# Weaving the steps of seven-product pairs, and making the FFN's token sums one stage earlier

## The chip, the cores and the metric

The kernel runs on one core of a Trainium2 chip. A core has a matmul engine (TensorE, PE in the profile, with its weight loads as PEld), a vector engine (VectorE, DVE), an activation engine (ScalarE, ACT), a general engine (GpSimd, POOL) and an engine that here only issues DMAs (SyncE, SP). Each engine works through its own queue of instructions in order, and semaphores make an instruction wait for another engine's. The metric is the time of one execution of the whole kernel on the device, in microseconds (us); lower is better.

## The reference

One encoder block on 256 tokens of width 2048, in fp32: RMSNorm, one wide projection, three attention mixers (A, B, C), a gate for each of them, an output projection, then a SwiGLU feed-forward network (FFN) with 5632 hidden columns. What matters here:

```
h = rms_norm(x, g_mix);  proj = h @ w_in          # queries, keys, values and 3 x 2048 gate columns
merged = sigmoid(gate0) * (oa @ w_br_a) + sigmoid(gate1) * (ob @ w_br_b) + sigmoid(gate2) * (oc @ w_br_c)
x = x + merged @ w_o
hf = rms_norm(x, g_ffn) @ w_ffn_in                # (2048, 2 x 5632)
x = x + (silu(hf[:, :5632]) * hf[:, 5632:]) @ w_ffn_out
```

## The kernel before

**Split products.** Every fp32 matrix is split into a rounded part and a rest, and one product of a 128x128 token tile with a 128x512 weight tile is three matmuls: hi x hi, hi x lo, lo x hi. The weights come from memory as tiles `raw` of 128 rows x (2 x 512) columns, 512 KB each, loaded by SP into a pool of six. ScalarE copies the rounded part (`whi`, L108), VectorE subtracts it from the weights (`wlo`, L109); both have four tiles. The function `halves` does that. So for every weight tile: DMA, ScalarE, VectorE, then TensorE, and a fifth split waits until TensorE is done with the first.

**Pairs.** From the gates on, the work goes by pairs of 512-column blocks (`pair`). The 2048 rows of a weight matrix are eight units of two 128-row tiles. In an ordinary unit each of the two blocks is one step of four products (12 matmuls). In a *seven-product pair* three of the eight units (the table `SEVEN`) are computed with seven products in place of eight, from sums of weights and sums of token tiles. The steps of a pair, with the letters used below (the number is the unit):

- d, D: an ordinary unit's first and second block; 12 matmuls each
- f: a seven-product unit's first step: loads two raw tiles, splits the first; products into the banks X and Y; 6 matmuls
- g: VectorE makes three weight sums (into t3, the second raw tile, t2; L428 to L430) and splits the result; products with token sums into W and Z; 6 matmuls
- h: VectorE makes one more sum in the first raw tile (L444) and half a split; one product into V; 3 matmuls
- p0, p2 and q0, q2: the sums t2 and t3 of all three units are split and multiplied with token sums into X; 6 and 3 matmuls

So a seven-product pair has 61 products, 183 matmuls. After the last f, ScalarE copies bank X to a tile SA; after the last g, bank W to SB; after p2, X again (L379). At the end of a pair VectorE adds banks and copies (L386, L387), while the next pair's steps go on. The token sums that g, p and q need (`stationary_forms`, tiles fh and fl) are six additions (L696), four differences (L699 to L702) and a split, made once for all gate pairs and once for all FFN pairs.

**Order.** A list of steps sets the order in a pair: `ORDER` (`d0 s4 d1 s5 d2 s6 6 d3 7 d7`, where s is f, g, h, and 6 and 7 are p and q) and `ORDER0` for the first gate pair and the first FFN pair. The splits of a step are issued three steps ahead of its matmuls (`AHEAD`). TensorE's and SP's queues keep the program's order; for ScalarE, VectorE and GpSimd the scheduler of the framework orders the queue by an estimated timeline and by priorities. Jobs on the side (evacuations, transposes, sums) advance one step after each step of a pair.

**Stages.** Pairs in order: four gate pairs (seven-product), each followed by an ordinary pair of a branch; two ordinary w_o pairs; the FFN in three blocks: four, four and three seven-product pairs, each block followed by two ordinary pairs of the output. Each 512 columns of the w_o output are added to x, squared and summed, and transposed into a token tile `x1T` of four k-tiles (L760, L111, L112); after the fourth one the token sums of the FFN are started (L764).

Of the kernel before, what the change touches and what calls it, by code (L numbers as in the profile page):

```python
# [57 lines left out]
class InOrder:  # L58

# [16 lines left out]
    def __init__(self, tc):  # L76
        self.tc, self.on = tc, False
        for name in ("tensor", "sync"):
            setattr(self, name, self._Engine(self, getattr(tc.nc, name)))
        for name in ("vector", "scalar", "gpsimd"):  # L80
            setattr(self, name, getattr(tc.nc, name))


@with_exitstack
def encoder_block(ctx: ExitStack, tc: tile.TileContext, a: dict, out: bass.AP):
# [244 lines left out]
    def halves(*srcs):  # L330

        hi = wp.tile([P, PK, NC], F32R, name="whi", bufs=4)
        lo = wp.tile([P, PK, NC], F32R, name="wlo", bufs=4)
        n = 0
        for v in srcs:
            if len(v.shape) == 2:
                split(hi[:, n], lo[:, n], v)
                n += 1
            else:
                split(hi[:, n:n + v.shape[1]], lo[:, n:n + v.shape[1]], v)  # L340
                n += v.shape[1]
        return hi, lo

    def pair(src, lhs, order, done, forms=None, operand=None):
# [33 lines left out]
        def copy(to, b):  # L378
            nc.scalar.activation(tl[to[0]][:, to[1]], ps[b], AF.Copy)  # L379
# [10 lines left out]
        def whole(u, c):  # L390
            def ready():
# [33 lines left out]
        def second(u):  # L425
            def ready():
                b1, b2 = held[u]
                nc.vector.tensor_add(t3[:, SEVEN.index(u)], b2[:, 0], b2[:, 1])  # L428
                nc.vector.tensor_add(b2[:, 0], b2[:, 0], b1[:, 0])
                nc.vector.tensor_add(t2[:, SEVEN.index(u)], b2[:, 0], b2[:, 1])  # L430
                hi, lo = halves(b2)

                def products():
                    mul("W", forms(u, 0), hi[:, 0], lo[:, 0])
# [4 lines left out]
            return ready

        def third(u):
            def ready():
                b1 = held.pop(u)[0]
                nc.vector.tensor_add(b1[:, 1], t2[:, SEVEN.index(u)], b1[:, 1])  # L444
# [24 lines left out]
        steps = []  # L469
        for o in order:  # L470
            u = int(o[1:] or 0)
            steps += {"d": lambda: [whole(u, 0), whole(u, 1)], "s": lambda: [first(u), second(u), third(u)],
                      "6": lambda: [rest("6", v) for v in range(0, seven, 2)],
                      "7": lambda: [rest("7", v) for v in range(0, seven, 2)]}[o[0]]()
# [27 lines left out]
    whole_k = lambda n: ["d%d" % u for u in range(n)]  # L502
# [205 lines left out]
    def merging():  # L708
        forms = stationary_forms(xT, tail)
        for b, (g0, k0, k1) in enumerate(((8, 2, 6), (4, 6, 12))):  # L710
            for j in (0, 2):
# [25 lines left out]
                yield pair(block_pair(a["w_gate"], g0 + j), xT, ORDER if b + j else ORDER0, gates, forms)  # L737
# [7 lines left out]
    def projecting():  # L745
# [4 lines left out]
        for n in (0, 2):  # L750
            def add(c, r, n=n):
# [4 lines left out]
                def later():  # L756
# [18 lines left out]
    def feeding():  # L775
        for c0, c1 in ((0, 4), (4, 8), (8, KF // 4)):
            hT = []
            for n in range(c0, c1):
# [19 lines left out]
                yield pair(lambda u, c, n=n: a["w_ffn"][n][2 * u + c], x1l, ORDER0 if n == 0 else ORDER, hidden,  # L798
# [107 lines left out]
```

## Time and profile before

| | |
|---|---|
| three runs, median (lowest to highest) | 1429.26 us (1427.81 to 1429.84) |
| the profiled execution | 1429.38 us, its span on the core 1427.6 us |
| granted TensorE clock, mean | 0.995 |
| data moved | 277.06 MB at a mean of 194 GB/s |

Stages by the profile's time, from the span's start: the three attention mixers and their projections until 377 us, gate and branch pairs until 607, the two w_o pairs until 698, then the FFN. A row of busy times by stretch gives the stretch, its length, then busy time and count of instructions for PE, PEld, DVE, ACT and POOL, the granted clock (1.00 is full), the DMA share and GB/s. A row of the timeline gives start, duration, engine, line, operation, tiles written and read, shapes, count, and in brackets the idle time before it with what ended it. A row of a group gives how often, the summed busy time, the mean in ns, and the idle time before. A row of waits gives the total, the number and the longest, in us. Buffer numbers are left out of tile names, so t2 and t3 both read t.

### The profile page before, as it was taken

The numbers are of one execution on the slowest core, as the hardware profiler recorded it, in microseconds if no ns is written. First come the engines' busy times: TensorE is split into PE (matmuls) and PEld (weight loads), VectorE is DVE, ScalarE is ACT, GpSimd is POOL, SyncE is SP. The second block draws the span as 40 slices with busy tenths as digits, with TensorE's granted clock in tenths as the row PEclk, the third lists the DMA queues.
The fourth block names the chain that finished last, engine by engine and source line by source line (L and its number), as shares of the span: only waits on it lengthen the run. The fifth ranks groups of instructions, "written<-read, shape, count | busy, mean of one in ns | idle before, by whom it ended". The sixth has DMA issues, their size and how long they took to land.

```text
span 1427.6 us, 17323 instructions
## 1 busy us (share of the span) xinstructions
PE 1397.1 (98%) x6287; PEld 1145.9 (80%) x6287; DVE 1026.0 (72%) x1305; ACT 767.6 (54%) x1026; POOL 76.6 (5%) x146
## 2 busy tenths in 40 slices
PE   8999999999999999999979999999999999999998
PEld 6778878888877888888858888888888888888886
DVE  5767756765578878755779987547988845788854
ACT  6766545654465564545456566335566643456632
POOL 0024532200000000000000000000000000000000
PEclk9999999999999999999999999999999999999999
DMA  8975535455555566755536656655565665565634
GB/s 295 335 243 197 158 123 173 163 163 193 175 192 192 182 219 188 264 179 184 170 119 207 208 188 215 185 190 192 197 199 180 225 189 191 180 201 188 220 128 174
DMA packets 79413, 277.06 MB, mean 194 GB/s; under 512 B 8992, under 2 KB 11552, under 8 KB 79072
## 3 DMA queue, kind: packets, MB, share of 16 engines
q1 hardware_dynamic: 79184, 275.94, 58.9%
q8 instruction: 49, 0.80, 0.2%
q14 instruction: 36, 0.29, 0.1%
q10 hardware_dynamic: 144, 0.02, 0.0%
HBM read 273.05 MB, written 2.88 MB: 193 GB/s over the span
## 4 chain that ended last, share of the span: by engine, by line
PE 83%; DVE 6%; DMA 5%; POOL 2%; issue 2%; ACT 2%; SPq 0%; DVEq 0%; ACTq 0%; POOLq 0%
PE mm L70 17%; PE mmZ L70 14%; PE mmV L70 14%; PE mmY L70 14%; PE mmQ L70 12%; PE mmX L70 6%; DVE wlo L109 3%; DMA raw<-in_w_gate 2%; PE mmW L70 2%; PE tp L70 1%; ACT whi L108 1%; DMA raw<-in_w_mem 1%; PE sc L70 1%; POOL rot L561 1%; DMA rows<-in_mem 1%
## 5 line engine op out<-in xcount | busy, mean ns | idle before, releaser
L109 DVE TENSOR_TENSOR wlo<-raw,whi 128x1024 fp32r<-128x1024 f32 (+1 forms) x541 | 636.9, 1191 | 305.7 <-ACT whi L108 303.5
L108 ACT ACTIVATE whi<-raw 128x1024 fp32r<-128x1024 f32 (+1 forms) x541 | 549.0, 1025 | 552.4 <-PE mmQ L70 159.3
L70 PE MATMUL mm<-whi,xT 128*128 128x512 f32 x768 | 244.8, 395 | 0.0
L70 PEld LDWEIGHTS mm<-whi,xT 128*128 128x128 f32 x768 | 144.6, 190 | 29.7 <-issue 0.8
L70 PE MATMUL mm<-wlo,xT 128*128 128x512 f32 x384 | 151.3, 394 | 0.0
L70 PE MATMUL mmY<-whi,x1T 128*128 128x512 f32 x286 | 112.4, 393 | 0.0
L70 PE MATMUL mmV<-whi,x1T 128*128 128x512 f32 x286 | 111.9, 391 | 0.0
L70 PE MATMUL mmZ<-whi,x1T 128*128 128x512 f32 x220 | 85.8, 390 | 0.0
L70 PE MATMUL mmQ<-whi,x1T 128*128 128x512 f32 x220 | 85.6, 389 | 0.0
L70 PEld LDWEIGHTS mm<-wlo,xT 128*128 128x128 f32 x384 | 72.8, 190 | 15.8 <-issue 0.8
L109 DVE TENSOR_TENSOR wlo<-t,whi 128x1024 fp32r<-128x1024 f32 (+1 forms) x60 | 55.9, 953 | 19.2 <-ACT whi L108 19.0
L70 PE MATMUL mmZ<-whi,hT 128*128 128x512 f32 x176 | 69.6, 396 | 0.0
L70 PE MATMUL mmQ<-whi,hT 128*128 128x512 f32 x176 | 69.1, 392 | 0.0
L70 PE MATMUL mmV<-whi,hT 128*128 128x512 f32 x176 | 69.0, 392 | 0.0
L70 PE MATMUL mmY<-whi,hT 128*128 128x512 f32 x176 | 69.0, 392 | 0.0
L70 PEld LDWEIGHTS mmV<-whi,x1T 128*128 128x128 f32 x286 | 54.0, 189 | 11.5
L70 PEld LDWEIGHTS mmY<-whi,x1T 128*128 128x128 f32 x286 | 53.9, 188 | 10.8
L108 ACT ACTIVATE whi<-t 128x1024 fp32r<-128x1024 f32 (+1 forms) x60 | 50.0, 841 | 13.7 <-PE mmQ L70 13.7
L70 PE MATMUL mmY<-wlo,x1T 128*128 128x512 f32 x143 | 56.0, 391 | 0.0
L70 PE MATMUL mmV<-wlo,x1T 128*128 128x512 f32 x143 | 55.9, 391 | 0.0
L428 DVE TENSOR_TENSOR t<-raw 128x512 f32<-128x512 f32 x45 | 31.1, 691 | 30.8 <-DMA raw<-in_w_ffn 15.4
L70 PEld LDWEIGHTS mmQ<-whi,x1T 128*128 128x128 f32 x220 | 41.3, 188 | 8.6
(252 smaller groups left out, 2548.8 us busy)
## 6 DMA issues: line engine op xcount, KB each, us to landing
raw<-in_w_ffn SPq DMA_DIRECT2D x176, 512.0 KB, 3.9
raw<-in_w_gate SPq DMA_DIRECT2D x96, 512.0 KB, 3.9
raw<-in_w_ffn_out SPq DMA_DIRECT2D x88, 512.0 KB, 3.6
raw<-in_w_qkv SPq DMA_DIRECT2D x64, 512.0 KB, 4.6
raw<-in_w_o SPq DMA_DIRECT2D x32, 512.0 KB, 3.6
raw<-in_w_br SPq DMA_DIRECT2D x24, 512.0 KB, 3.7
raw<-in_w_mem SPq DMA_DIRECT2D x16, 512.0 KB, 6.7
rawT<-in_memT SPq DMA_DIRECT2D x8, 256.0 KB, 5.2
```

Source lines behind the costliest of these rows:

```text
L70: ins = op(*args, **kw)
L108: nc.scalar.activation(hi, src, AF.Copy)
L109: nc.vector.tensor_sub(lo, src, hi.bitcast(F32))
L428: nc.vector.tensor_add(t3[:, SEVEN.index(u)], b2[:, 0], b2[:, 1])
L561: op(ov[:, :, :, c], ov[:, :, :, c], tmp[:, :n])
```

## The change

- `SEVEN` is (1, 2, 3) in place of (4, 5, 6), and the order lists now name single steps, so that f, g, h of a unit can stand apart, with d or D steps of other units between. There are three lists: one for the first gate pair, one for the first FFN pair, one for all others.
- `follow`: splits of weights and sums of weights on VectorE, and splits on ScalarE, each get a dependency on the one issued before on the same engine, so that these keep the program's order. The scheduler places everything else around them.
- The copies of banks X and W are issued with high priority.
- The FFN's token sums are started after the second 512 columns of w_o, since units 1 to 3 need only token tiles 2 to 7.

```diff
-SEVEN = (4, 5, 6)
-ORDER = "d0 s4 d1 s5 d2 s6 6 d3 7 d7".split()
-ORDER0 = "d0 d1 d2 s4 d3 s5 s6 6 7 d7".split()
+SEVEN = (1, 2, 3)
+STEPS = "d0 f1 D0 g1 d4 h1 f2 D4 g2 d5 h2 f3 D5 g3 d6 h3 p0 p2 D6 q0 q2 d7 D7".split()
+STEPS_GATE = "d0 D0 d4 D4 f1 d5 g1 D5 h1 f2 g2 d6 h2 f3 g3 h3 p0 p2 D6 q0 q2 d7 D7".split()
+STEPS_FFN = "d0 D0 f1 d4 g1 D4 h1 f2 d5 g2 D5 h2 f3 d6 g3 h3 p0 p2 D6 q0 q2 d7 D7".split()
...
+    def follow(self, ins):
+
+        if self.on:
+            last = self.before.get(ins.ins.engine)
+            if last is not None:
+                self.tc.add_manual_dep(ins.ins, last, mybir.DependencyInfo(mybir.DependencyClass.NoSync,
+                                                                           mybir.DependencyReason.DATA),
+                                       reason="follow")
+            self.before[ins.ins.engine] = ins.ins.name
...
-            if len(v.shape) == 2:
-                split(hi[:, n], lo[:, n], v)
-                n += 1
-            else:
-                split(hi[:, n:n + v.shape[1]], lo[:, n:n + v.shape[1]], v)
-                n += v.shape[1]
+            v = v.unsqueeze(1) if len(v.shape) == 2 else v
+            o = slice(n, n + v.shape[1])
+            nc.follow(nc.scalar.activation(hi[:, o], v, AF.Copy))
+            nc.follow(nc.vector.tensor_sub(lo[:, o], v, hi[:, o].bitcast(F32)))
+            n += v.shape[1]
...
         def copy(to, b):
-            nc.scalar.activation(tl[to[0]][:, to[1]], ps[b], AF.Copy)
+            with tc.high_priority():
+                nc.scalar.activation(tl[to[0]][:, to[1]], ps[b], AF.Copy)
...
-                    if u + 1 < len(order):
+                    if 2 * u + 2 < KT:
...
-                nc.vector.tensor_add(t3[:, SEVEN.index(u)], b2[:, 0], b2[:, 1])
-                nc.vector.tensor_add(b2[:, 0], b2[:, 0], b1[:, 0])
-                nc.vector.tensor_add(t2[:, SEVEN.index(u)], b2[:, 0], b2[:, 1])
+                nc.follow(nc.vector.tensor_add(t3[:, SEVEN.index(u)], b2[:, 0], b2[:, 1]))
+                nc.follow(nc.vector.tensor_add(b2[:, 0], b2[:, 0], b1[:, 0]))
+                nc.follow(nc.vector.tensor_add(t2[:, SEVEN.index(u)], b2[:, 0], b2[:, 1]))
...
-                yield pair(block_pair(a["w_gate"], g0 + j), xT, ORDER if b + j else ORDER0, gates, forms)
+                yield pair(block_pair(a["w_gate"], g0 + j), xT, STEPS if b + j else STEPS_GATE, gates, forms)
...
-                    if n + c == 3:
+                    if n + c == 1:
                         forms.append(stationary_forms(x1l))
+                    elif n + c == 3:
                         yield 2
...
-                yield pair(lambda u, c, n=n: a["w_ffn"][n][2 * u + c], x1l, ORDER0 if n == 0 else ORDER, hidden,
+                yield pair(lambda u, c, n=n: a["w_ffn"][n][2 * u + c], x1l, STEPS if n else STEPS_FFN, hidden,
```

The places in the queues that matter, before and in the changed kernel. The line numbers move by 10 to 13 (L108 becomes L121 or, in `halves`, L351; L109 becomes L122 or L352).

ScalarE in the first gate pair, before, from the split of h5 to that of q2 (the tiles t_3605 and t_3606 are t2 and t3):

```order
L108 ACTIVATE whi<-raw 128x512
L108 ACTIVATE whi<-raw 128x1024 x2
L379 ACTIVATE SA<-mmX 128x512
L108 ACTIVATE whi<-raw 128x512
L108 ACTIVATE whi<-t_3605 128x1024
L108 ACTIVATE whi<-t_3605 128x512
L379 ACTIVATE SB<-mmW 128x512
L108 ACTIVATE whi<-t_3606 128x1024
L108 ACTIVATE whi<-t_3606 128x512
```

and in the changed kernel, from the split of h2 to that of D6:

```order
L351 ACTIVATE whi<-raw 128x512
L351 ACTIVATE whi<-raw 128x1024
L392 ACTIVATE SA<-mmX 128x512
L351 ACTIVATE whi<-raw 128x1024
L351 ACTIVATE whi<-raw 128x512
L351 ACTIVATE whi<-t_3605 128x1024
L392 ACTIVATE SB<-mmW 128x512
L351 ACTIVATE whi<-t_3605 128x512
L351 ACTIVATE whi<-raw 128x1024
```

The copy of X now stands between the splits of f3 and g3, no longer behind that of g6, and a split of raw (D6) stands between those of t2 and t3.

VectorE where the FFN's token sums end, before, in the first FFN pair (ffull are the six sums, fraw the differences, fl the split's rest):

```order
L699 TENSOR_TENSOR fraw<-ffull 128x384
L109 TENSOR_TENSOR wlo<-raw,whi 128x1024
L428 TENSOR_TENSOR t_6054<-raw 128x512
L701 TENSOR_TENSOR fraw<-fraw,ffull 128x384
L429 TENSOR_TENSOR raw<-raw 128x512
L702 TENSOR_TENSOR fraw<-fraw,ffull 128x384
L430 TENSOR_TENSOR t_6053<-raw 128x512
L109 TENSOR_TENSOR fl<-fraw,fh 128x1536
L109 TENSOR_TENSOR wlo<-raw,whi 128x1024 x2
```

and in the changed kernel, in the second w_o pair:

```order
L706 TENSOR_TENSOR ffull<-x1T 128x256
L709 TENSOR_TENSOR fraw<-ffull 128x384
L352 TENSOR_TENSOR wlo<-raw,whi 128x1024
L711 TENSOR_TENSOR fraw<-fraw,ffull 128x384
L712 TENSOR_TENSOR fraw<-fraw,ffull 128x384
L352 TENSOR_TENSOR wlo<-raw,whi 128x1024
L122 TENSOR_TENSOR fl<-fraw,fh 128x1536
L352 TENSOR_TENSOR wlo<-raw,whi 128x1024 x7
```

The sums now stand among the splits of w_o weights; the split fl is followed by seven splits of weights, of w_o and of the first FFN pair, and only then by the additions of the last w_o blocks to x.

VectorE at the start of the third FFN pair (t_6840 is t3, t_6839 is t2, hT the evacuated transposes of the pair before), before:

```order
L386 TENSOR_TENSOR SB<-mmZ,SB 128x512
L387 TENSOR_TENSOR SB<-mmQ,SB 128x512
L444 TENSOR_TENSOR raw<-t_6839,raw 128x512
L428 TENSOR_TENSOR t_6840<-raw 128x512
L109 TENSOR_TENSOR wlo<-raw,whi 128x1024
L793 TENSOR_TENSOR SA<-SA,SB 128x1024
L429 TENSOR_TENSOR raw<-raw 128x512
L109 TENSOR_TENSOR wlo<-raw,whi 128x512
L109 TENSOR_TENSOR wlo<-raw,whi 128x1024
L430 TENSOR_TENSOR t_6839<-raw 128x512
```

and in the changed kernel:

```order
L399 TENSOR_TENSOR SB<-mmZ,SB 128x512
L400 TENSOR_TENSOR SB<-mmQ,SB 128x512
L442 TENSOR_TENSOR raw<-raw 128x512
L804 TENSOR_TENSOR SA<-SA,SB 128x1024
L443 TENSOR_TENSOR t_6839<-raw 128x512
L352 TENSOR_TENSOR wlo<-raw,whi 128x1024 x2
L457 TENSOR_TENSOR raw<-t_6839,raw 128x512
L122 TENSOR_TENSOR hT<-tp,hT 128x512
L352 TENSOR_TENSOR wlo<-raw,whi 128x512
L352 TENSOR_TENSOR wlo<-raw,whi 128x1024 x2
```

Before, the sums of the next unit (L428, L429) and the sum for h (L444) ran ahead of splits that stand earlier in the program; now each stands between the splits of its neighbouring steps.

More of the change, by code (lines that the diff above doesn't have):

```diff
@@ L76, in __init__ @@
     def __init__(self, tc):
-        self.tc, self.on = tc, False
+        self.tc, self.on, self.before = tc, False, {}
         for name in ("tensor", "sync"):
@@ L335, in halves @@
         for v in srcs:
-            if len(v.shape) == 2:
-                split(hi[:, n], lo[:, n], v)
-                n += 1
-            else:
-                split(hi[:, n:n + v.shape[1]], lo[:, n:n + v.shape[1]], v)
-                n += v.shape[1]
+            v = v.unsqueeze(1) if len(v.shape) == 2 else v
[3 more added lines that the diff above has]
+            n += v.shape[1]
         return hi, lo
     def pair(src, lhs, order, done, forms=None, operand=None):
-        seven = sum(o[0] == "s" for o in order)
+        seven = sum(o[0] == "f" for o in order)
         left = {"X": 3 * seven}
         for o in order:
-            for b in {"s": "YZWV", "d": "YVZQ" * 2}.get(o[0], ""):
+            for b in {"f": "Y", "g": "WZ", "h": "V", "d": "YV" * 2, "D": "ZQ" * 2}.get(o[0], ""):
                 left[b] = left.get(b, 0) + 1
@@ L443, in ready @@
                 b1 = held.pop(u)[0]
-                nc.vector.tensor_add(b1[:, 1], t2[:, SEVEN.index(u)], b1[:, 1])
+                nc.follow(nc.vector.tensor_add(b1[:, 1], t2[:, SEVEN.index(u)], b1[:, 1]))
                 hi, lo = halves(b1[:, 1])
@@ L449, in rest @@
         def rest(o, v):
-            tt, f = {"6": (t2, 1), "7": (t3, 3)}[o]
+            tt, f = (t2, 1) if o == "p" else (t3, 3)
             n = min(2, seven - v)
@@ L459, in products @@
                     if v + n == seven:
-                        if o == "6":
+                        if o == "p":
                             copy(("B", 0), "X")
@@ L467, in rest @@
             return ready
[L469 to L474, printed above, removed]
+        kinds = {"d": lambda u: whole(u, 0), "D": lambda u: whole(u, 1), "f": first, "g": second, "h": third,
+                 "p": lambda v: rest("p", v), "q": lambda v: rest("q", v)}
+        steps = [kinds[o[0]](int(o[1:])) for o in order]
         for i, ready in enumerate(steps):
@@ L500, in run @@
         nc.on = False
-    whole_k = lambda n: ["d%d" % u for u in range(n)]
+    whole_k = lambda n: [d + str(u) for u in range(n) for d in "dD"]
     block_pair = lambda w, n: lambda u, c: w[n + c][u]
```

## The prediction

> **What bounds the kernel now.** I read the page first, then TensorE's own waits, then the busy time of each stretch between two pairs, then the rows around the longest wait.
>
> ```profile
> span 1427.6 us, 17323 instructions
> PE 1397.1 (98%) x6287; PEld 1145.9 (80%) x6287; DVE 1026.0 (72%) x1305; ACT 767.6 (54%) x1026; POOL 76.6 (5%) x146
> ...
> 781.80 2.04 PE mmX L70 x9
> ```
>
> TensorE is the bound, but its 98% counts matmuls that overlap. The last row, from the chain of waits, is the better measure: nine matmuls in 2.04 us, 0.2267 us each when nothing waits. A seven-product pair has 61 products of three matmuls, 183, so its floor is 41.49 us, plus its transposes. Each stretch below is one pair: the four gate pairs, the second w_o pair, FFN pairs 0, 2 and 10.
>
> ```profile
> 377.25:423.12 45.87, 43.10 (x185) 33.89 (x183) 35.36 (x42) 24.53 (x29) 0.00 (x0) 1.00 0.55 174
> 434.00:477.27 43.27, 41.88 (x184) 34.28 (x183) 34.68 (x41) 24.80 (x29) 0.00 (x0) 1.00 0.57 188
> 488.15:530.69 42.54, 41.94 (x184) 34.20 (x183) 34.69 (x41) 24.80 (x29) 0.00 (x0) 1.00 0.59 192
> 547.01:590.48 43.47, 43.47 (x201) 35.85 (x199) 36.97 (x45) 26.74 (x33) 0.00 (x0) 1.00 0.60 193
> 652.57:698.34 45.77, 45.77 (x210) 37.63 (x208) 25.34 (x29) 22.49 (x32) 0.00 (x0) 1.00 0.57 184
> 698.34:753.64 55.30, 46.53 (x201) 36.86 (x199) 45.07 (x75) 29.26 (x40) 0.00 (x0) 0.94 0.42 134
> 796.60:839.28 42.68, 42.68 (x193) 35.06 (x191) 36.88 (x44) 25.20 (x31) 0.00 (x0) 1.00 0.60 192
> 1313.18:1355.63 42.45, 42.45 (x193) 35.13 (x191) 36.08 (x42) 26.12 (x32) 0.00 (x0) 1.00 0.62 207
> ```
>
> The first number is the length, the third busy time that of VectorE (DVE), the fourth that of ScalarE (ACT). FFN pair 10 (eight transposes, 42.45) has no wait that matters; pair 2 has 0.23. So the FFN's ordinary pairs can give almost nothing. What can be won: gate pairs 45.87, 43.27 and 42.54 against 41.49, so 4.4, 1.8 and 1.1; the fourth (16 transposes, 2.0 more) nothing; and FFN pair 0, 55.30 against 41.49 and about 1.8 for 16 transposes: 12.0. The waits say what ends them:
>
> ```profile
> PE mmW L70 <- ACT fh L108: 6.8, 1, 6.8
> PE mmY L70 <- DVE wlo L109: 2.7, 4, 1.4
> PE mmX L70 <- ACT SB L379: 1.9, 2, 0.9
> ```
>
> ```profile
> 717.74 0.39 PE L70 MATMUL mmY<-whi,x1T 128*128 128x512 f32 x1
> 724.92 0.79 PE L70 MATMUL mmW<-whi,fh 128*128 128x512 f32 x1 [6.79 <-ACT fh L108]
> ...
> 728.58 0.63 PE L70 MATMUL mmV<-whi,x1T 128*128 128x512 f32 x1
> 729.01 0.63 PE L70 MATMUL mmV<-wlo,x1T 128*128 128x512 f32 x1
> ...
> 730.30 0.39 PE L70 MATMUL mmY<-whi,x1T 128*128 128x512 f32 x1
> 730.53 0.39 PE L70 MATMUL mmV<-whi,x1T 128*128 128x512 f32 x1
> ```
>
> In FFN pair 0 TensorE stands from 717.74 to 724.92 because the token sums (tile fh) are made late; the next matmuls start 0.43 us apart (728.58 to 729.01) instead of 0.23. The nine matmuls from 724.92 to 729.83 took 4.9 us instead of 2.04. Wait (6.95) and slow spell (2.87) cost 9.8 of the 12.0; the other 2.2 are short waits near the pair's end.
>
> **The change part by part.** No matmul, load or sum is added or removed; TensorE's floor stays. The changed bound on the operand fetch in the first pair means the same eight units, so that stage stays as it is.
>
> *Token sums.* The six additions, four differences and the split move from FFN pair 0 into the second w_o pair.
>
> ```profile
> L109 DVE TENSOR_TENSOR wlo<-raw,whi 128x1024 fp32r<-128x1024 f32 x31 | 37.9, 1223 | 25.5 <-ACT whi L108 25.2
> L696 DVE TENSOR_TENSOR ffull<-x1T 128x256 f32<-128x256 f32 x6 | 2.5, 418 | 0.0
> L701 DVE TENSOR_TENSOR fraw<-fraw,ffull 128x384 f32<-128x384 f32 x1 | 0.6, 554 | 0.0
> L109 DVE TENSOR_TENSOR fl<-fraw,fh 128x1536 fp32r<-128x1536 f32 x1 | 1.8, 1757 | 0.9 <-ACT fh L108 0.9
> L108 ACT ACTIVATE fh<-fraw 128x1536 fp32r<-128x1536 f32 x1 | 1.5, 1482 | 4.1 <-DVE fraw L702 4.1
> ```
>
> That is 2.5 + 4 x 0.55 + 1.76 = 6.5 us of VectorE and 1.5 of ScalarE. The w_o pair has VectorE busy 25.34 of 45.77 us and ScalarE 22.49, so 20 and 23 idle: hidden, 0. Were that cover gone, 6.5. Nothing waits behind them: in the new order the last of them, the split into fh and fl, stands after the eleventh of this pair's sixteen weight splits. Gain: 9.8, all of it if the new first FFN pair has its operands. It reaches token tiles 8 and 9 at its fourth step (d4), before at its seventh:
>
> ```profile
> 703.63 0.48 DVE L112 SCALAR_TENSOR_TENSOR x1T<-tp,gT,x1T 128x256 fp32r<-128x256 f32 x1
> 704.65 0.49 DVE L112 SCALAR_TENSOR_TENSOR x1T<-tp,gT,x1T 128x256 fp32r<-128x256 f32 x1
> ```
>
> These two are ready at 705.1 even in the old queue. The new pair needs them after d0, D0, f1 and three transpose groups: 698.34 + 2.72 + 2.72 + 1.36 + 3 x 0.4 = 706.4. Cover 1.3 us; cost 0.
>
> *Prices for the queues.* Rows of one tail of FFN pair 2, and two of its DVE work:
>
> ```profile
> 822.73 0.39 PE L70 MATMUL mmW<-whi,fl 128*128 128x512 f32 x1
> ...
> 821.18 1.06 ACT L108 ACTIVATE whi<-t 128x1024 fp32r<-128x1024 f32 x1 [0.90 <-PE mmQ L70]
> 822.14 0.58 ACT L379 ACTIVATE SA<-mmX 128x512 f32<-128x512 f32 x1
> 822.62 0.62 ACT L108 ACTIVATE whi<-t 128x512 fp32r<-128x512 f32 x1
> 823.16 0.60 ACT L379 ACTIVATE SB<-mmW 128x512 f32<-128x512 f32 x1
> ...
> 804.94 0.68 DVE L430 TENSOR_TENSOR t<-raw 128x512 f32<-128x512 f32 x1
> 805.54 1.22 DVE L109 TENSOR_TENSOR wlo<-raw,whi 128x1024 fp32r<-128x1024 f32 x1
> 806.68 0.68 DVE L109 TENSOR_TENSOR hT<-tp,hT 128x512 fp32r<-128x512 f32 x1
> ...
> 822.27 1.83 DVE L109 TENSOR_TENSOR wlo<-t,whi 128x1024 fp32r<-128x1024 f32 x2 [1.27 <-ACT whi L108]
> ```
>
> VectorE advances by 0.60 for 512 columns and 1.14 for 1024. ScalarE advances by 0.96 and 0.48, hands over 0.03 after its end (822.24 to 822.27), and copies a bank 0.43 after the start of its last matmul (822.73 to 823.16). I put 0.12 on a VectorE sum that ScalarE waits for, an estimate between that 0.03 and 0.43. On TensorE d and D take 2.72, f, g, p0 and q0 1.36, h, p2 and q2 0.68.
>
> *First gate pair.* The new order has f3, g3, h3, p0 in a row, and ScalarE's row shows the SA copy before g3's split. From f3's start: X's last matmul starts at 0.45, the copy at 0.88, g3's whi at 1.36 to 2.42, its wlo 2.45 to 3.67. TensorE wants g3 at 1.36: wait 2.27 (the wlo is first needed by the second matmul). Then h3 needs an addition (0.60), 0.12, whi 0.62, wlo 0.69: 0.7 late; p0, behind h3 on both engines, 0.8 late. Sum 3.8 against 4.4 now: gain 0.6. So this pair hardly profits, though D6 now stands between p2 and q0 and covers the SB copy (the 1.9 of the third wait row).
>
> *Other gate pairs.* Their waits now sit at D3, d2 and the like, where VectorE was late. In the new order I followed VectorE from the pair's start: eight ops of the merge (4.8) fall before g1, then g1, d4, h1, f2, D4 follow at 1.14 to 2.95 each. It reaches g2 0.13 late and g3, whose two sums, hand-over, whi and wlo take 3.6 against TensorE's 2.72 for D5, 0.45 late; the end 0.07. So 0.65 for pairs two and three (1.8 and 1.1 now: gains 1.1 and 0.4), and 0.5 for the fourth, which has none now: loss 0.5.
>
> *FFN pair 0.* Its tail f3, d6, g3, h3, p0 has d6 between, so g3 is in time; h3 0.5 and p0 0.8 late as above, g2 0.3. 1.6 in place of 2.2: gain 0.6.
>
> *FFN pairs 1 to 10.* VectorE's busy time stays at 36 to 37 of 42.5. What is new is that weight sums and splits keep one sequence, so a sum whose data are there no longer runs ahead. Followed from the pair's start as above, with transposes of the previous pair inside: g2 is 0.3 us early, g3 0.15 late in the eight pairs with transposes, nothing in the two that follow an output pair. 1.2 in all, against about 1.6 now (0.2 to 0.5 in pairs 1, 2, 3, 7 and 9): gain 0.4.
>
> *Loads.* f takes two of the six raw tiles and keeps one until h, now four steps later instead of two. In the new program a load waits for the split five or six steps earlier, before six or seven.
>
> ```profile
> raw<-in_w_ffn SPq DMA_DIRECT2D x176, 512.0 KB, 3.9
> ...
> 443.91 5.76 DMA raw<-in_w_gate
> ```
>
> The tightest is D5, issued when D4's wlo ends; ScalarE asks for it about 7.6 us later. 3.9 at the median, 5.8 the longest piece on the chain: hidden, 0.
>
> Sum: 9.8 + 0.6 + 1.1 + 0.4 - 0.5 + 0.6 + 0.4 = 12.4; I take 12.0, since the small terms rest on waits of tenths. The profiled execution took 1429.38 (the span of 1427.6 and 1.8 around it), so 1417.4. The median of three is 0.12 lower: **1417.3**. Bounds: if every wait of the walk vanished (3.8 + 1.3 + 0.5 + 1.6 + 1.2 = 8.4), 1409; if the token sums alone gained and every other pair lost 0.6, 1425.
>
> **The rivals.** *A, forecast: 1417.3.* Between 1415 and 1420.
>
> *B: the weaving clears the tails too.* For it: VectorE is idle 6 us in each pair. Against: the copy stands before g3 in ScalarE's queue. Half of the 8.4: 1413.
>
> *C: the fixed sequence costs more.* Every sum now waits for the split before it. If VectorE enters each pair 0.6 later than I walked it, the 13 pairs after the first gate pair and FFN pair 0 lose 0.6 each: 7.8, 1425. Against: their VectorE idle time.
>
> *D: the clock.* A gap of 7.18 us was followed by matmuls 0.43 apart. The first gate pair now has one wait of 2.3; if that is enough, it starts a slow spell like the one from 724.92 (nine matmuls with 0.2 us extra each, 1.8): 1419.1. [...]
>
> *E: slower.* Loads come too late. Place: D4, D5, d6 of each pair; price: each us past the 7.6 delays D5's wlo, and with it, in fixed order, all sums behind it. At a landing of 8.1 us, 0.5 in 39 units: 19.5 more than the forecast, 1437. It decides from 7.6; the longest seen is 5.8.
>
> *F: the gain of FFN pair 0 is not there.* The sums are early, but the token tiles of the third w_o block are late by the same 9.8: 1427. Against: the cover of 1.3.
>
> **How the numbers follow.** A 0.55, B 0.12, C 0.17, D 0.06, E 0.05, F 0.05. The range leaves out B's lower half, C's upper half, E and F, together 0.2: 1412 to 1424. For this kernel 0.2% (2.9 us) is about what can be told from no change. Faster (under 1426.4): A, B, D and most of C, 0.88. Same: a quarter of C, and most of F, 0.07. Slower: E, 0.05.
>
> **What would show it.** FFN pair 0 about 45 us long, without the wait on fh and without matmuls 0.43 apart. The second w_o pair still 45.8. The first gate pair about 45.3, with one wait of some 2.3 us before mmW near its end and shorter ones at mmV and mmX. FFN pairs 1 to 10 within 0.3 of 42.5. I am wrong if the first gate pair comes near 42 (B), if ordinary pairs are 43 or more (C), if matmuls wait for DMA (E), or if the fourth step of FFN pair 0 waits for x1T (F).

## The result, and the profile after

The changed kernel takes 1418.5 us (median of four runs, 1417.93 to 1419.69) against 1429.26 (1427.81 to 1429.84, four runs): a ratio of 0.9927, 95% interval 0.991 to 0.9945. It is faster by 10.8 us, close to the forecast of 1417.3. The profiled executions differ by 9.7 us (1429.38 and 1419.69; the spans are 1427.6 and 1417.9).

The head of the page of the changed kernel, then the busy time by stretch, for the same eight stretches as in the prediction: the four gate pairs, the second w_o pair, FFN pairs 0, 2 and 10:

```profile
span 1417.9 us, 17330 instructions
PE 1395.6 (98%) x6287; PEld 1144.8 (81%) x6287; DVE 1033.6 (73%) x1305; ACT 764.9 (54%) x1026; POOL 76.7 (5%) x146
```

```profile
377.32:423.07 45.75, 44.03 (x184) 35.10 (x183) 36.07 (x42) 24.65 (x29) 0.00 (x0) 0.96 0.58 174
433.95:476.16 42.21, 41.90 (x185) 34.27 (x183) 37.02 (x44) 24.43 (x29) 0.00 (x0) 1.00 0.62 199
487.04:529.26 42.22, 41.88 (x184) 34.28 (x183) 37.01 (x44) 24.43 (x29) 0.00 (x0) 1.00 0.62 198
545.58:589.32 43.74, 43.74 (x201) 35.85 (x199) 39.28 (x48) 26.37 (x33) 0.00 (x0) 1.00 0.60 198
651.41:697.18 45.77, 45.77 (x210) 37.64 (x208) 31.45 (x40) 23.87 (x33) 0.00 (x0) 1.00 0.58 184
697.18:742.34 45.16, 44.29 (x200) 35.79 (x199) 39.57 (x64) 29.19 (x41) 0.00 (x0) 1.00 0.53 174
785.22:828.09 42.87, 42.74 (x192) 35.06 (x191) 37.95 (x45) 25.59 (x32) 0.00 (x0) 1.00 0.62 195
1303.06:1345.94 42.88, 42.76 (x192) 35.06 (x191) 37.93 (x45) 25.61 (x32) 0.00 (x0) 1.00 0.60 197
```

By these pairs nearly the whole gain is one row: FFN pair 0 went from 55.30 to 45.16 us. The second w_o pair carries the token sums now (VectorE 31.45 us busy, before 25.34) and still takes 45.77. The first gate pair hardly moved (45.87 to 45.75), and its granted clock is 0.96, where it was 1.00 before. FFN pairs 2 and 10 are longer than before (42.68 and 42.45). Branch and output pairs are the same to 0.05 us.

### The profile page after: what moved, and what is told of

It reads as the page before. It is cut to its first block, busy times and chain, and to the rows that moved or that the text cites. A ratio compares the mean times of both kernels' runs of the same rounds, so it can differ in the third digit from the quotient of the medians.

```text
span 1417.9 us, 17330 instructions
## 1 busy us (share of the span) xinstructions
PE 1395.6 (98%) x6287; PEld 1144.8 (81%) x6287; DVE 1033.6 (73%) x1305; ACT 764.9 (54%) x1026; POOL 76.7 (5%) x146
## 4 chain that ended last, share of the span: by engine, by line
PE 84%; DVE 5%; ACT 3%; issue 3%; DMA 2%; POOL 2%; SPq 0%; ACTq 0%; DVEq 0%; POOLq 0%
PE mm L73 17%; PE mmZ L73 15%; PE mmV L73 14%; PE mmY L73 14%; PE mmQ L73 13%; PE mmX L73 6%; DVE wlo L352 3%; ACT whi L351 2%; PE mmW L73 2%; DMA raw<-in_w_mem 1%; PE tp L73 1%; PE sc L73 1%; POOL rot L571 1%; DVE raw L442 1%; DVE t L441 1%
## 5 line engine op out<-in xcount | busy, mean ns | idle before, releaser
L352 DVE TENSOR_TENSOR wlo<-raw,whi 128x1024 fp32r<-128x1024 f32 (+1 forms) x441 | 509.6, 1168 | 249.1 <-ACT whi L351 245.0
L351 ACT ACTIVATE whi<-raw 128x1024 fp32r<-128x1024 f32 (+1 forms) x441 | 437.4, 1013 | 403.0 <-PE mmV L73 133.7
L122 DVE TENSOR_TENSOR wlo<-raw,whi 128x1024 fp32r<-128x1024 f32 x100 | 128.5, 1295 | 80.8 <-ACT whi L121 80.6
L121 ACT ACTIVATE whi<-raw 128x1024 fp32r<-128x1024 f32 x100 | 105.7, 1070 | 88.1 <-PE mm L73 81.4
L73 PE MATMUL mmV<-whi,x1T 128*128 128x512 f32 x286 | 108.6, 392 | 0.0
L73 PEld LDWEIGHTS mmY<-whi,x1T 128*128 128x128 f32 x286 | 53.7, 188 | 11.3
L352 DVE TENSOR_TENSOR wlo<-t,whi 128x1024 fp32r<-128x1024 f32 (+1 forms) x60 | 54.7, 953 | 3.9 <-ACT whi L351 3.9
L351 ACT ACTIVATE whi<-t 128x1024 fp32r<-128x1024 f32 (+1 forms) x60 | 48.5, 834 | 0.0
```

Source lines behind the costliest of these rows:

```text
L73: ins = op(*args, **kw)
L121: nc.scalar.activation(hi, src, AF.Copy)
L122: nc.vector.tensor_sub(lo, src, hi.bitcast(F32))
L351: nc.follow(nc.scalar.activation(hi[:, o], v, AF.Copy))
L352: nc.follow(nc.vector.tensor_sub(lo[:, o], v, hi[:, o].bitcast(F32)))
```

## The experiments

Each is the changed kernel with one edit, unless it says otherwise. Ratios are against the kernel before, on the same chip, with their 95% interval; the length of a pair is read between the starts of the first matmuls of neighbouring pairs.

**1. The token sums alone, in the kernel before.**

```diff
-SEVEN = (4, 5, 6)
-ORDER = "d0 s4 d1 s5 d2 s6 6 d3 7 d7".split()
+SEVEN = (1, 2, 3)
+ORDER = "d0 s1 d4 s2 d5 s3 6 d6 7 d7".split()
...
-                    if n + c == 3:
+                    if n + c == 1:
                         forms.append(stationary_forms(x1l))
```

The first gate pair gets the list `d0 d4 d5 s1 d6 s2 s3 6 7 d7`, FFN pair 0 the one above.

> The kernel before with one part of the change alone: the seven-product pairs are 1, 2 and 3, and the token sums start in the first w_o pair; no step is woven, no high priority, no following. Theory A (my terms: the gain is the wait of 6.95 us on the token sums and the 2.87 us that the slow matmuls behind it cost): 55.30 us of FFN pair 0 become 42.7 to 45.5, everything else stays within 0.5 us a pair, so the time is about 1419 us (1417 to 1421). Rival (the weaving brings the gain, the early sums only move the wait elsewhere): FFN pair 0 keeps 52 us or more, or the w_o pairs grow by what it loses, and the time is above 1426 us.

1425.18 us (1420.84 to 1430.63), ratio 0.9969 (0.9954 to 0.9983). Neither theory: FFN pair 0 took 50.96 us:

```profile
697.16:748.12 50.96, 45.27 (x201) 37.04 (x200) 38.38 (x62) 29.27 (x40) 0.00 (x0) 0.97 0.46 147
```

The wait on fh is gone, but in its place TensorE stood 2.8 us before f1's first matmul and 2.9 before a transpose, both for splits of token tiles (x1T), which hold the banks that come next. That is the rival F of the prediction, with another cause: the tiles' source was there, their splits stood late in ScalarE's and VectorE's queues. So the early sums by themselves are worth 4.3 us in this pair, not 10.

**2. The weaving, with sums started late.** The start of the sums goes back behind the last w_o half, and FFN pair 0 gets three whole units ahead of its first f.

```diff
-STEPS_FFN = "d0 D0 f1 d4 g1 D4 h1 f2 d5 g2 D5 h2 f3 d6 g3 h3 p0 p2 D6 q0 q2 d7 D7".split()
+STEPS_FFN = "d0 D0 d4 D4 d5 D5 f1 g1 h1 f2 d6 g2 h2 f3 D6 g3 h3 p0 p2 q0 q2 d7 D7".split()
...
-                    if n + c == 1:
+                    if n + c == 3:
                         forms.append(stationary_forms(x1l))
```

> The changed kernel with the token sums started again behind the last w_o half, and in FFN pair 0 an order in which three whole pairs stand ahead of the first seven-product step, as before, so that the sums are asked for at the same 78th group of matmuls. Theory A: the wait of some 7 us on the sums returns, and a slow spell of 2 to 3 us behind it; FFN pair 0 takes 53 to 56 us against 45.2, all other pairs stay as in the changed kernel, and the time is about 1428 us (1426 to 1430). Rival (weaving is what helps): FFN pair 0 stays under 49 us and the time under 1423 us. Rival on the clock (the slow matmuls of the kernel before had nothing to do with the wait): the wait returns, the slow spell does not, FFN pair 0 takes 52 to 53 us and the time is about 1425.5 us.

1425.49 us (1423.27 to 1430.12), ratio 0.9973 (0.9963 to 0.9983); FFN pair 0 took 52.66 us. A little less than I expected: the waits on fh and fl were 2.6 and 1.4 us, not 7. The time is what the rival on the clock gives, but not for its reason: eight slow matmuls follow the waits (721.67 to 725.09). Units 1 to 3 need only token tiles of the first w_o pair, so the six additions ran one behind the other (from 703.69 us of that trace), though they were started late. Part of the gain thus comes from which units have seven products, not from when the sums start: against run 3, which differs in the units alone, it is 2.0 us. Run 3 undoes both.

**3. Units 4 to 6 and late sums again, all else as changed.**

```diff
-SEVEN = (1, 2, 3)
+SEVEN = (4, 5, 6)
...
-                    if n + c == 1:
+                    if n + c == 3:
                         forms.append(stationary_forms(x1l))
```

In the three lists units 1 to 3 and 4 to 6 change places; FFN pair 0 has the list of run 2 so renamed.

> The changed kernel with only the token sums' part undone: the seven-product units are 4, 5 and 6 again, as before, the sums start behind the last w_o half, and FFN pair 0 asks for them at the same 78th group of matmuls as before; weaving, sequence and priority stay. Theory A (the sums need token tiles of the last w_o halves, which is what the 6.95 us wait and the slow spell came from): FFN pair 0 takes 53 to 57 us against 45.2, the other pairs stay as in the changed kernel within 0.3 us, and the time is 1426 to 1430 us. Rival (the fixed sequence alone brings the sums forward, since no weight sum stands ahead of them): FFN pair 0 takes 46 to 50 us, 1419 to 1423 us.

1427.29 us (1425.81 to 1430.16), ratio 0.9984 (0.997 to 0.9999). Its waits of TensorE, and the stretch of FFN pair 0:

```profile
PE mmW L73 <- ACT fh L121: 3.0, 1, 3.0
PE mmW L73 <- DVE fl L122: 1.9, 1, 1.9
PE mmX L73 <- ACT SB L392: 1.0, 1, 1.0
```

```profile
695.35:749.96 54.61, 48.02 (x201) 37.50 (x199) 45.79 (x75) 30.50 (x42) 0.00 (x0) 0.94 0.46 144
```

Theory A holds: the wait is back (3.0 and 1.9 us, not the 6.95 of the kernel before), twelve matmuls 0.43 us apart follow it, FFN pair 0 takes 54.61 us against 45.16, and the other pairs stay within 0.15 us. The token sums' part is worth 9.5 us by that pair and 8.8 by the medians; the prediction had 9.8. But some 1.1 of it is not the sums: the list that this run has in FFN pair 0 puts q0 right behind p2, and q0 waits for the copy SB (third row). In the list of the changed kernel D6 stands between the two.

**4. The weaving alone undone.** Sums early and one sequence for halves and sums, but f, g, h and d, D side by side:

```diff
-STEPS = "d0 f1 D0 g1 d4 h1 f2 D4 g2 d5 h2 f3 D5 g3 d6 h3 p0 p2 D6 q0 q2 d7 D7".split()
+STEPS = "d0 D0 f1 g1 h1 d4 D4 f2 g2 h2 d5 D5 f3 g3 h3 p0 p2 d6 D6 q0 q2 d7 D7".split()
```

and the other two lists likewise.

> The changed kernel with the weaving alone undone: sums of the tokens early, halves and weight sums still in one sequence, but the three steps f, g, h of a seven-product unit and the two half pairs d, D stand side by side in the three lists. Theory A (a fixed sequence needs the weaving: f then gives g only 1.36 us of cover, and g3 behind f3 cost 2.15 us in the first gate pair of the changed kernel): 0.8 to 2.2 us at each of three g a pair, so 44 to 48 us in place of 42 to 43 in each ordinary pair, and 1440 to 1490 us in all. Rival (the sequence alone does it, the weaving adds nothing): pairs of 42.5 to 43 us, 1417 to 1421 us.

1448.55 us (1447.49 to 1449.73), ratio 1.0125 (1.0096 to 1.0154): 30 us above the changed kernel, inside the range of theory A, though the waits are not at g. FFN pair 2:

```profile
801.27:845.76 44.49, 43.36 (x192) 34.88 (x191) 37.95 (x45) 25.06 (x32) 0.00 (x0) 1.00 0.60 192
```

It takes 44.49 us, and TensorE stands at h2, at the d5 behind it and at p0: h's addition waits for the splits of f and g on VectorE, and TensorE reaches h 2.7 us after f's start. FFN pair 0 takes 54.80 us, again on splits of token tiles; those 9.6 of the 30 us are not the lost cover that theory A speaks of. The other 20 are spread over the 14 other seven-product pairs (1.2 to 1.9 each).

**5. The sequence alone undone** (no `follow`; scheduler's order for halves and weight sums, as before):

```diff
-            nc.follow(nc.scalar.activation(hi[:, o], v, AF.Copy))
-            nc.follow(nc.vector.tensor_sub(lo[:, o], v, hi[:, o].bitcast(F32)))
+            nc.scalar.activation(hi[:, o], v, AF.Copy)
+            nc.vector.tensor_sub(lo[:, o], v, hi[:, o].bitcast(F32))
```

and so for the weight sums.

> The changed kernel without the fixed sequence of halves and weight sums: each engine takes them in the order in which the scheduler puts them, as before. Theory A (the fixed sequence helps: without it VectorE reaches additions of the next seven-product step ahead of their loads, and work that TensorE needs stands behind them): pairs get uneven, FFN pairs at 42.5 to 43.4 as in the kernel before and in the run with the sums alone, FFN pair 0 at 47 to 51, and the time about 1421 to 1426 us. Rival C of the prediction (the fixed sequence costs, it is what makes g3 0.40 us late): the FFN pairs fall to 42.45, FFN pair 0 stays at 45, and the time is about 1415 us.

1432.33 us (1427.01 to 1436.56, ten runs), ratio 1.002 (1.0002 to 1.0037): 13.8 us above the changed kernel by the medians, more than I expected. The profiled execution, at 1436.39, is one of the slow end. VectorE's waits for loads, in the kernel before and in this run; the changed kernel has no such row:

```profile
DVE t L428 <- DMA raw<-in_w_ffn: 15.4, 23, 1.8
DVE t L428 <- DMA raw<-in_w_gate: 15.0, 11, 2.9
```

```profile
DVE t L441 <- DMA raw<-in_w_ffn: 26.3, 22, 2.6
DVE t L441 <- DMA raw<-in_w_gate: 18.0, 11, 3.7
```

The columns are the total, the times and the longest. Without the sequence VectorE takes the first sum of the next seven-product unit before its load has landed, and everything behind it in its queue waits too. In the woven lists this costs 44 us of VectorE, some of which TensorE feels. Its longest row of waits in this run, and the place in FFN pair 2:

```profile
PE mmZ L73 <- DVE wlo L352: 12.2, 9, 1.9
...
820.66 0.69 DVE L441 TENSOR_TENSOR t<-raw 128x512 f32<-128x512 f32 x1 [1.82 <-DMA raw<-in_w_ffn]
```

The split that D6 needs stands behind this sum and its two neighbours, ends at 823.94, and D6's second matmul starts at 823.99, 1.3 us late. FFN pairs 1, 2, 4, 5, 6, 8 and 9 take 43.3 to 44.6 us for this reason, 1.4 to 2.2 at D6 each; their g3 is on time, so rival C of the prediction is right about that place. Elsewhere it goes both ways: FFN pair 0 takes 51.0 us, the fourth gate pair 48.10 (43.73 with the sequence; transposes stand behind such a sum), the first gate pair only 42.40 (45.75). Another 3.7 us of the profiled execution are in the last output pair, which waits for a load of its own weights; no run shows whether the missing sequence has a part in that.

**6. Which addition holds g3 in the ordinary pairs.** In the changed kernel g3 comes 0.40 us late in eight FFN pairs. VectorE and, last row, ScalarE in FFN pair 5 (L441 makes t3, L442 the sum that g3's half reads, L443 t2):

```profile
1023.36 0.69 DVE L441 TENSOR_TENSOR t<-raw 128x512 f32<-128x512 f32 x1
1024.09 0.69 DVE L442 TENSOR_TENSOR raw<-raw 128x512 f32<-128x512 f32 x1
1024.81 0.69 DVE L443 TENSOR_TENSOR t<-raw 128x512 f32<-128x512 f32 x1
...
1024.86 2.01 ACT L351 ACTIVATE whi<-raw 128x1024 fp32r<-128x1024 f32 x2 [0.74 <-DVE raw L442]
```

ScalarE stands idle 0.74 us until the second sum is there. The edit makes that sum first and t3 last, from t2:

```diff
-                nc.follow(nc.vector.tensor_add(t3[:, SEVEN.index(u)], b2[:, 0], b2[:, 1]))
                 nc.follow(nc.vector.tensor_add(b2[:, 0], b2[:, 0], b1[:, 0]))
                 nc.follow(nc.vector.tensor_add(t2[:, SEVEN.index(u)], b2[:, 0], b2[:, 1]))
+                nc.follow(nc.vector.tensor_sub(t3[:, SEVEN.index(u)], t2[:, SEVEN.index(u)], b1[:, 0]))
```

> The changed kernel with the three weight sums of a seven-product step in another sequence: the sum that the step's own rounded half reads comes first, and t3 comes last, as t2 less the first half, so the half of g3 is released one addition (0.69 us) earlier. Theory A (the 0.40 us wait at g3 in nine FFN pairs and 0.60 in two gate pairs is VectorE being one addition late, while ScalarE stands idle for 0.74 us ahead of that half): the waits at g3 fall to 0 to 0.1 us in these pairs, the FFN pairs with transposes go from 42.87 to 42.5 us and the two gate pairs lose 0.5 each; in all 3.5 to 4.5 us less, about 1414.3 us. Rival 1 (ScalarE's copy of the finished chain, put ahead by its high priority, is what holds g3): nothing changes, 1418.5 us. Rival 2 (the wait goes to the next step, since h3 and p0 hang on the same VectorE): g3 gains 0.4 and h3 or p0 loses as much, 1417.5 to 1419 us.

1418.47 us (1417.1 to 1419.18), ratio 0.9916 (0.9904 to 0.9929): no change in all, and yet theory A is right where it was aimed. The same place with the edit (start of that pair 0.20 us earlier):

```profile
1022.63 0.69 DVE L441 TENSOR_TENSOR raw<-raw 128x512 f32<-128x512 f32 x1
...
1023.83 2.00 ACT L351 ACTIVATE whi<-raw 128x1024 fp32r<-128x1024 f32 x2
```

The half starts 1.03 us earlier and ScalarE no longer waits. The eight FFN pairs with transposes take 42.45 us each (before 42.87), gate pairs two and three 41.56 (42.2): 4.7 us. The first gate pair gave 1.4 more. But FFN pair 0 took 49.91 us in place of 45.16, and the fourth gate pair 0.4 more. In FFN pair 0 (ScalarE, VectorE, TensorE):

```profile
699.74 1.06 ACT L351 ACTIVATE whi<-raw 128x1024 fp32r<-128x1024 f32 x1 [1.44 <-issue]
700.70 0.82 ACT L124 ACTIVATE x1T<-tp,gT 128x256 fp32r<-128x256 f32 x2
...
700.83 1.23 DVE L352 TENSOR_TENSOR wlo<-raw,whi 128x1024 fp32r<-128x1024 f32 x1 [0.60 <-ACT whi L351]
...
702.64 0.87 DVE L125 SCALAR_TENSOR_TENSOR x1T<-tp,gT,x1T 128x256 fp32r<-128x256 f32 x2
...
703.66 0.47 PE L73 MATMUL mmX<-whi,x1T 128*128 128x512 f32 x1 [3.57 <-DVE rs_t L137]
```

With the sum earlier, the scheduler puts two halves of weights (of g1 and of D4) ahead of the second split of a token tile. The latter half waits 1.44 us, until D0's last matmul has read the tile that it is to fill; the token tile's split waits behind it on ScalarE and then behind the rest `wlo` on VectorE. The bank that it reads is the one mmX needs (the profile names the small operation that ended last before it). TensorE stands 3.57 us, and six slow matmuls and four slow transposes follow (the granted clock is 0.54 from 704.40 to 707.81).

**7. Cover for g3 in the first gate pair.** First d6 is moved behind f3:

```diff
-STEPS_GATE = "d0 D0 d4 D4 f1 d5 g1 D5 h1 f2 g2 d6 h2 f3 g3 h3 p0 p2 D6 q0 q2 d7 D7".split()
+STEPS_GATE = "d0 D0 d4 D4 f1 d5 g1 D5 h1 f2 g2 h2 f3 d6 g3 h3 p0 p2 D6 q0 q2 d7 D7".split()
```

> The changed kernel with one token moved in the first gate pair's list: d6 stands between f3 and g3 and no longer ahead of h2. Theory A (the two gaps of 1.34 and 1.26 us in the first gate pair stand there because g3 follows f3 directly, and they set off the eight matmuls of 0.427 us): both gaps and the slow spell go, the pair falls from 45.75 us to 42.3 to 43.0, and the time by 2.8 to 3.4 us, to about 1415.4 us. Rival 1 (VectorE and ScalarE are behind in this pair whatever the order): the gaps move to h2 and f3, the pair stays at 44.5 us or more and the time at 1417.5 or more. Rival 2 (the slow spell has a cause of its own): the gaps go, the eight slow matmuls stay, the pair takes 43.8 to 44.6 us and the time is about 1417 us.

1418.45 us (1416.99 to 1423.17), ratio 0.9923 (0.9909 to 0.9936). The pair took 45.53 us: rival 1. The two long gaps are gone, but h2, f3, g3, h3 and p0 now lose 0.6 to 0.9 us each. One step of cover moved is not one won. Then the steps of FFN pair 0 (`d0 D0 f1 d4 g1 D4 h1 f2 d5 g2 D5 h2 f3 d6 g3 h3 p0 p2 D6 q0 q2 d7 D7`) in the first gate pair too, one d or D between f and g throughout:

> The changed kernel with the steps of FFN pair 0 in the first gate pair (f1 third, d6 between f3 and g3, one d or D between f and g throughout). Theory A (the first gate pair is slow because its steps f2, g2 and f3, g3 stand side by side): g2 and g3 find a step of 2.72 us ahead of them, the two gaps and the slow matmuls go, only h3 and p0 keep 0.5 and 0.8 as in FFN pair 0; 42.8 us (42.3 to 43.3) in place of 45.75, all else as it was, the time about 1415.6 us. Rival (as in the run with d6 moved: the work of this pair is late on VectorE and ScalarE whatever the order): 44.5 us or more.

A single run of 1415.54 us; the pair took 42.60 us, as theory A has it, and only h3 and p0 waited.

**8. The copies without priority.**

```diff
         def copy(to, b):
-            with tc.high_priority():
-                nc.scalar.activation(tl[to[0]][:, to[1]], ps[b], AF.Copy)
+            nc.scalar.activation(tl[to[0]][:, to[1]], ps[b], AF.Copy)
```

> The changed kernel without the high priority of the copies out of the finished chains. Theory A (the priority only moves a copy of 0.6 us ahead of one split of ScalarE, and matters just where ScalarE is the late one, at g3 in the first gate pair): that pair gains or loses up to 1 us, all others stay within 0.2 us, 1417.5 to 1419.5 us. Rival (the priority is what keeps D6 and q0 from waiting for the bank of X): p0 and q0 wait 0.5 to 1 us in each of the 15 seven-product pairs, 7 to 15 us more, 1425 to 1433 us.

1418.66 us (1416.69 to 1419.19), ratio 0.9923 (0.9908 to 0.9938), no difference. The priority is worth nothing that these runs can tell. The run shows something else. The same two gaps stand in its first gate pair, and the clock stays full. TensorE and the granted clock (the number ahead of the DMA share) in stretches of 3.41 us, changed kernel first:

```profile
404.04:407.46 3.42, 1.70 (x7) 0.89 (x6) 2.91 (x4) 1.54 (x2) 0.00 (x0) 1.00 0.26 107
407.46:410.87 3.41, 3.41 (x10) 2.31 (x9) 2.40 (x4) 3.06 (x5) 0.00 (x0) 0.53 0.65 178
410.87:414.28 3.41, 3.41 (x16) 2.80 (x16) 3.29 (x5) 3.32 (x5) 0.00 (x0) 0.97 0.55 149
```

```profile
404.57 0.39 PE L73 MATMUL mmY<-whi,xT 128*128 128x512 f32 x1
405.91 0.49 PE L73 MATMUL mmW<-whi,fh 128*128 128x512 f32 x1 [0.95 <-ACT whi L351]
407.17 0.50 PE L73 MATMUL mmW<-wlo,fh 128*128 128x512 f32 x1 [0.77 <-DVE wlo L352]
...
407.81 0.63 PE L73 MATMUL mmZ<-whi,fh 128*128 128x512 f32 x1
408.24 0.63 PE L73 MATMUL mmZ<-wlo,fh 128*128 128x512 f32 x1
```

and in the run without priority:

```profile
401.73:405.14 3.41, 2.02 (x7) 1.23 (x7) 2.20 (x4) 1.46 (x3) 0.00 (x0) 1.00 0.19 29
405.14:408.56 3.42, 2.67 (x10) 1.68 (x10) 3.04 (x4) 3.42 (x5) 0.00 (x0) 1.00 0.78 255
```

```profile
401.03 0.39 PE L73 MATMUL mmY<-whi,xT 128*128 128x512 f32 x1
402.36 0.50 PE L73 MATMUL mmW<-whi,fh 128*128 128x512 f32 x1 [0.94 <-ACT whi L351]
403.62 0.50 PE L73 MATMUL mmW<-wlo,fh 128*128 128x512 f32 x1 [0.76 <-DVE wlo L352]
...
404.20 0.39 PE L73 MATMUL mmZ<-whi,fh 128*128 128x512 f32 x1
404.43 0.39 PE L73 MATMUL mmZ<-wlo,fh 128*128 128x512 f32 x1
```

The gaps are 1.34 and 1.26 us in both. With the slow spell the pair takes 45.75 us, without it 45.53. The spell costs 0.2, since eight slow matmuls (1.6 us) fill the time in which h3 and p0 would have waited (0.6 and 0.8). With the same steps and a spell the pair took 46.03 us in run 2 and 45.89 in run 3, so 0.2 to 0.5. In the three traces without that spell (this run and both of section 7) the second gate pair takes 42.5 us in place of 42.2, so over both pairs the cost is smaller still; the reason for these 0.3 is open.

**9. The findings together.** The steps of FFN pair 0 in the first gate pair, and t3 last in all pairs but FFN pair 0:

> The changed kernel with the sequence of sums of the run on the sum order (t3 last, as t2 less the first half) in every pair but FFN pair 0, where t3 stays first, and with the steps of FFN pair 0 in the first gate pair too. Theory A: the 4.75 us that FFN pair 0 lost in that run came only from the queues there, where two splits of weights stood ahead of the second split of a token tile; with the old sequence in this pair it takes 45.2 again, while gate pairs two and three keep 41.56 and FFN pairs 1 to 10 their 42.45 (41.49 without transposes). With 42.8 in the first gate pair the span is 1417.9 - 2.9 - 1.3 - 3.4 = 1410.3 and the time about 1412 us (1410 to 1414). Rival 1 (FFN pair 0 waits on token tiles by chance, run by run): 49 to 51 us there again, about 1417 us. Rival 2 (shorter pairs ahead bring loads too late): some matmuls wait for DMA, above 1416 us.

1408.77 us (1407.93 to 1410.45), ratio 0.9854 (0.9838 to 0.9871): it beats both kernels, is 9.7 us below the changed one by the medians, and 1.2 below the range of theory A, since the first gate pair took 41.56 us and not 42.8. The four gate pairs, then FFN pairs 0 and 2:

```profile
375.92:417.48 41.56, 41.56 (x185) 34.36 (x183) 35.70 (x42) 24.56 (x29) 0.00 (x0) 1.00 0.61 191
428.36:469.92 41.56, 41.56 (x185) 34.36 (x183) 36.91 (x44) 24.38 (x29) 0.00 (x0) 1.00 0.62 203
480.80:522.36 41.56, 41.56 (x185) 34.36 (x183) 36.91 (x44) 24.38 (x29) 0.00 (x0) 1.00 0.63 203
538.68:582.76 44.08, 43.66 (x200) 35.84 (x199) 39.00 (x48) 26.48 (x33) 0.00 (x0) 1.00 0.60 196
690.61:735.72 45.11, 44.22 (x200) 35.79 (x199) 39.57 (x64) 29.19 (x41) 0.00 (x0) 1.00 0.53 173
778.17:820.62 42.45, 42.45 (x193) 35.13 (x191) 37.86 (x45) 25.54 (x32) 0.00 (x0) 1.00 0.61 197
```

Three gate pairs and all FFN pairs from 1 on now stand at the shortest length that any run showed. With t3 first for the first unit of each pair and last for the other two, FFN pair 0 among them:

> The run with sums and gate order once more, but t3 stands first for the first of the three units in every pair, FFN pair 0 among them, and last for the other two. Theory A (only g2 and g3 hang on that addition; for the first unit the earlier sum only pushes splits of transposed tiles back): the fourth gate pair goes from 44.09 to 43.6 us, the tail of FFN pair 0 gives 0 to 1 us, all others stay at their floors; 0.5 to 1.5 us less than that run's 1408.8, about 1407.8 us. Rival (the order of g1 counts too): the ordinary pairs lose 0.1 to 0.4 each again, 1410 to 1413 us.

1410.31 us (1408.97 to 1410.74), ratio 0.9858 (0.9835 to 0.9882). The fourth gate pair fell to 43.49 us and FFN pair 0 to 44.91, 0.8 together, and the other pairs stay at their floors, as theory A has it. The time lies in the range of the rival, though not for its reason; the two totals, taken on different chips, do not tell the versions apart.

## Why the prediction was right, and where it was not

**Token sums** (predicted gain 9.8, and 0.6 from FFN pair 0's tail): right for the whole change. 55.30 to 45.16 us is 10.1; the undo of run 3 gives 9.5, and 8.4 without q0's wait. The w_o pair hid them, and x1T's cover held in this queue. But the early sums alone gave 4.3 in this pair (run 1); the term counts as theirs what only came with the new queues. That the cover held was luck of the queue rather than the 1.3 us I worked out (706.34 less 705.14 is 1.2): in runs 1, 4, 5 and 6 the same pair waited on splits of token tiles. My argument asked when the splits are ready in the old queue; the question was what the scheduler puts ahead of them in the new one. The tail's waits are h3 0.54 and p0 0.79, as walked (0.5 and 0.8); the 0.3 at g2 did not come.

**First gate pair** (45.3 predicted, 45.75 measured): the chain from f3 to the copy to g3 ran as walked. The copy started 0.88 us after f3's start, the two gaps lost 2.15 us (2.27 predicted). What I gave little chance (rival D) happened: a slow spell. It did not cost the 1.8 us I had priced, but 0.2 against run 8, because the waits behind it shrank. Another 0.2 were lost at g2, where my walk had nothing.

**Other gate pairs** (predicted 1.1 and 0.4 gained, 0.5 lost): 1.06 and 0.31 gained, 0.26 lost. Right in place and about in size.

**FFN pairs 1 to 10** (gain 0.4): this step failed. They lost 1.6 us in sum (424.4 to 426.0). The step was "g3 0.15 late in the eight pairs with transposes"; it is 0.40. The mechanism, VectorE's sums in front of g3's half, was right, and run 6 confirms it. The size was off since I let all sums advance by 0.60 us, read from two rows where the second did not need the first. Sums that touch each other's tiles advance by 0.72 (1023.36 to 1024.09 to 1024.81). From the start of the first sum to the end of g3's first rest `wlo` the walk had 3.6 us; the rows of run 6 give 3.81 (1023.36 to 1027.17: that `wlo` starts at 1025.95 and takes 1.22). That is 0.2 of the 0.25 missing, and as much is missing in the gate pairs (g3 0.61 and 0.65 late, 0.45 predicted); the rest is open.

**The fixed sequence** (only rival C spoke of it, as a cost): the direction was wrong. Without it the woven lists are 13.8 us slower (run 5), and without the weaving the fixed sequence is 30 us slower (run 4). With the sums early there are four cases, since run 1 has the lists of run 4: neither 1425.2 us, the sequence alone 1448.6, the weaving alone 1432.3, both 1418.5. So each alone costs, 23 and 7 us, and the two together gain 6.7. They do not gain it in the ordinary pairs: FFN pairs 1 to 10 take 425.7, 441.3, 435.4 and 426.0 us in sum. FFN pair 0 takes 50.96, 54.80, 51.01 and 45.16, and these 5.8 us are most of the gain, in the one pair whose length hung on what the scheduler put ahead of the token tiles. The number came out because I walked the final order. The profile before had a row that shows what the sequence also does: 30.4 us in which VectorE waited for a load at its first weight sum. The prediction does not use it. I had written that a sum whose data are there no longer runs ahead; the sequence also holds back the sum whose data are not there.

**Loads** (0): right; no wait of TensorE or VectorE for a weight load from the gates on; ScalarE's are in the last output pair, 11.3 us against 10.6 before. **The sum:** 10.1 + 0.1 + 1.1 + 0.3 - 0.3 - 1.6 = 9.7, which is what the two profiled executions differ by. The terms of the forecast add up to 12.4, cut to 12.0: 1.6 + 0.4 too much in the FFN pairs, 0.5 in the first gate pair. The medians differ by 1.1 more than the profiled executions, which brought the time nearer to the forecast than the working was. Two figures do not follow from the working: what the range leaves out adds up to 0.245, not 0.2, and the bound of 1425 is the forecast plus 13 x 0.6; with the token sums as the only gain it would be 1427.

## What to carry to other kernels

In an engine that works in order, look at which instruction can stand at the head of the queue waiting for data: an early sum that waits for a load stops everything behind it (44 us of VectorE in run 5), and fixing the sequence pays when the order is also laid out to give each step cover. Undo such a pair of measures one by one and both together: here each alone made the kernel slower. When several results feed one consumer chain, make first the one that the next engine reads. And after any local win, look at the whole table of stages: a reordered queue gave 4.7 us in ten pairs and took 4.8 back in one.

## What the runs showed of the hardware

A slow spell needs no long gap. In the changed kernel the longest gap in the first gate pair is 1.34 us between starts, and the granted clock is 0.50 from 407.64 to 411.06 us. In the kernel before, a gap of 1.34 us in the same pair (from 414.17) was followed by a granted clock of 1.00, the one of 7.18 us in FFN pair 0 by 0.50 from 722.95 to 729.77. Away from the start and the end of the program each of the two traces has one more such stretch, from 196.02 to 199.43 and, before, from 193.88 to 200.71. So the slow stretches last 3.41, 3.42, 6.83 and 6.82 us: one length of 3.413 (a sixth of their sum) or two. In the changed kernel they start 211.62 us apart, in the kernel before 529.07, which are 62.0 and 155.0 times that length.

Nor does TensorE have to stand still ahead of a slow stretch. From 404.04 to 407.46 us of the changed kernel five matmuls of 128x512 start, where fifteen fit at 0.2267 us each, and the next 3.41 us run at a granted clock of 0.53; in the run without priority seven start from 401.73 to 405.14, around the same gaps, and the clock stays at 1.00. Other stretches of this length: none start from 719.54 in the kernel before, with 0.50 behind it; three from 700.98 in run 6, with 0.54 behind it; in run 1 four and four transposes from 702.13 and nine from 705.55, both with 1.00 behind them, then only three from 708.96 to 712, and 0.52 from 712.37. Why nearly the same gaps set off a spell in one trace and none in another is not shown. The start of the gate stage varies from 373.8 to 377.3 us between the traces: 377.32 in the changed kernel and 377.25 in the kernel before, with the slow stretches near 195 us, and 373.81 in the run without priority, whose mean granted clock is 1.000. The eight slow matmuls of a stretch of 3.41 us cost 1.6 us; that this is part of the run-to-run spread of some 2 us is my estimate.

VectorE's additions of 128x512 start 0.60 us apart when independent (546.12, 546.72 and 547.32 us in the changed kernel) and 0.72 when the second reads or overwrites a tile of the first (1023.36, 1024.09 and 1024.81, the three sums of run 6), though each lasts 0.68 to 0.69 in both cases.
